# Sixty MLP units of a float32 decoder layer, from three matmuls per weight block to a two-matmul form with a PSUM bank of its own

## The chip, the core and the metric

The kernel runs on one core of a Trainium2 chip. The metric is the device time of one execution in microseconds (us): the median of several runs, beside runs of the kernel before. The engines are TensorE (PE in the profile, its weight loads PEld), VectorE (DVE), ScalarE (ACT) and SyncE (SP), which here issues the loads of weights. GpSimd does nothing.

## What is computed

One decoder layer on 256 tokens of width 2048, all in float32. The change lies in its last part, the MLP with a squared ReLU and a gated residual add:

```python
h2 = _modulate(_rms_norm(x, norm2_g[l]), shift2, scale2)
ff = jnp.square(jax.nn.relu(jnp.einsum("bsd,df->bsf", h2, w_ff1[l])))
x = x + gate2[:, None, :] * jnp.einsum("bsf,fd->bsd", ff, w_ff2[l])
return _rms_norm(x, final_g)
```

`w_ff1` is 2048 x 8192 and `w_ff2` 8192 x 2048.

## The kernel before

**Two halves of a float32.** TensorE is given float32 data rounded to its faster float32 form (`F32R`). To keep the precision, a number is held as a rounded part and the rest: ACT rounds (`w_round`, L178), DVE subtracts to get the rest (`w_rest`, L183). A product of weight and activation is then three products: rounded weight by rounded activation, rounded weight by the activation's rest, and the weight's rest by the rounded activation. The fourth is left out.

**Units.** A unit makes 128 output features for all 256 tokens. It has 16 blocks of 128 x 128 weights, one load of 1 MB, rounded and split in two halves of 128 x 1024 (`wh`, `wl`, four buffers each). There are two forms of it on TensorE:

- `gemm` (L196, matmuls at L204 to L206): three matmuls of 256 columns for each block, all added into one half of a PSUM bank (128 x 256 float32). 48 matmuls.
- `gemm_wide` (L221, matmuls at L229 to L232): one matmul of 512 columns takes the rounded weight to both halves of the activation at once, into both halves of a bank, and one of 256 columns adds the weight's rest to the first half. 32 matmuls. The result is the sum of the bank's halves. `join=True` adds them with an ACT copy (L236) and a DVE add (L237); with `join=False` the caller adds them to the residual with two DVE instructions.

**The MLP in four chunks.** Chunk c makes 16 tiles of `ff` (the first items, `ff1_unit`) and then adds what they give to the 16 tiles of the residual (`ff2_unit`). In the chunks c = 1, 2, 3 the first eight output tiles of the second product are not made in units but in summed steps (`sum_step`, matmuls at L1086 to L1088): a scheme that needs 7 products of blocks in place of 8, on sums of tokens (`token_sums`, L978 to L981) and sums of weights (`Item.sum`, L1010 to L1012). A step has 21 matmuls of 256 columns. There are 16 steps in a chunk; one stands behind each unit from f = 3 of the first items to f = 10 of the second product. The sums are held in PSUM for the whole chunk: 14 products, two to a bank, in the four banks of the pool `pa` and in three of the four banks of the pool `pg`. So while steps run, one bank is left for the units.

**The hand-written order.** In these chunks the function `mlp` (L1021) sets the order of all four engines; `pin` keeps it as the program order. `items` holds units and steps in the order of TensorE. While item i runs on TensorE, item i + 2 is rounded and split: `round` and `rest` of its first half, `round` and `rest` of its second half, and if the item behind it is a step, that step's sums of weights. Between these stand the three actions of the unit itself, `done[0]`, `done[1]` and `done[2]`. The rounding of a half waits until TensorE has used the buffer that it is written to: for a unit, those of the unit before (the first half when that is half done, the second half when it ends).

- A first item's actions are: ReLU out of PSUM into SBUF on ACT (L1137, `done[0]`, ahead of the second `round`), square and rounding on ACT (L1141, L1142, `done[1]`), the rest on DVE (L1146, `done[2]`, behind the second `rest`).
- A second item (f = 8, 9, 10) has one: its sum goes from PSUM into the residual (L1154, `done[2]`, behind the second `rest`).

The units f = 11 and up of the second product run outside `mlp`, in the common loop with a scheduler's order; f = 11 is a `gemm` too, f = 12 to 15 are wide or, at the very end, cut in pieces (`last_units`). `half_of` gives two neighbouring units the two halves of one bank (a bank each for f < 4 of the first items). Behind the third chunk DVE also joins the 14 sums (L1063, L1103, L1112) and squares are summed for the last norm (L157 to L161).

Of the kernel before, what the change touches and what calls it, by code (L numbers as in the profile page):

```python
# [10 lines left out]
F32 = mybir.dt.float32  # L11
# [55 lines left out]
def hybrid_layer(ctx: ExitStack, tc: tile.TileContext, x, xt, wada, w_p, w_r, w_f, vec, lruw, relb,  # L67
# [15 lines left out]
    def nm(s):  # L83
        cnt[0] += 1
        return f"{s}{cnt[0]}"
# [134 lines left out]

    def gemm_wide(parts, acts, join=True, out=None):  # L221

        ps = pg.tile([P, 2, T], F32, tag="pg", name=nm("pg"))
        n = len(acts)
        for k, hl in enumerate(acts):
            wh, wl = parts[k * P // WCH]
            w = slice(k * P % WCH, k * P % WCH + P)
            if k > 0:
                te.matmul(ps[:, 0], lhsT=wl[:, w], rhs=hl[:, 0], start=False, stop=False)  # L229
            te.matmul(ps, lhsT=wh[:, w], rhs=hl, start=k == 0, stop=k == n - 1)  # L230
            if k == 0:
                te.matmul(ps[:, 0], lhsT=wl[:, w], rhs=hl[:, 0], start=False, stop=False)  # L232
        if not join:
# [756 lines left out]
    class Item:  # L990
# [17 lines left out]
        def sum(self):  # L1008
            r = self.sums
            pin(ve.tensor_tensor(out=r[:, 4:6], in0=r[:, 1:3], in1=r[:, 0:1].broadcast_to((P, 2, T)), op=ALU.subtract))  # L1010
            pin(ve.tensor_tensor(out=r[:, 6], in0=r[:, 2], in1=r[:, 4], op=ALU.add))
            pin(ve.tensor_tensor(out=r[:, 7], in0=r[:, 6], in1=r[:, 3], op=ALU.subtract))  # L1012
# [8 lines left out]
    def mlp(items, ready, n):  # L1021
# [5 lines left out]
        for i, it in enumerate(items[:end]):  # L1027
# [4 lines left out]
            new.rest()  # L1032
            if not it.step and soon and soon.step:
                soon.sum()
            if not it.step:
                it.done[0](ps)
            new.round()
            if not it.step:
# [83 lines left out]

    hb = [None]

    def half_of(f, own=False):
        if own or f % 2 == 0:
            hb[0] = pg.tile([P, 2, T], F32, tag="pg", name=nm("pg"))
        return hb[0][:, f % 2]

    chunk = []  # L1130

    def first_item(c, f):
        t = {}

        def relu(ps):
            t[0] = tmp()
            pin(se.activation(t[0][:, 0], ps, AF.Relu))  # L1137

        def square(_):
            hl = ff[c, f] = pair(F32R)  # L1140
            pin(se.activation(t[0][:, 1], t[0][:, 0], AF.Square))  # L1141
            pin(se.activation(hl[:, 0], t[0][:, 1], AF.Copy))  # L1142
# [5 lines left out]
        def run(w):  # L1148
            return gemm(w, 0, [zn[k] for k in range(KT)], half_of(f, f < 4), pin)
        return Item(run, (relu, square, rest, [f // 2] if f % 2 else None), next_src())  # L1150

    def second_item(c, f):
        def out(ps):
            pin(ve.scalar_tensor_tensor(out=x1[f], in0=ps, scalar=mod[:, 5 * KT + f:5 * KT + f + 1], in1=x1[f],  # L1154
                                        op0=ALU.mult, op1=ALU.add))
            if c == 3:
                last_square(f)

        def run(w):
            return gemm(w, 0, [ff[c, j] for j in range(16)], half_of(f), pin)  # L1160
        return Item(run, (same, same, out, None), next_src())

# [115 lines left out]
    def ff2_unit(c, f):  # L1278
        def run(w):
# [5 lines left out]
            if c == 0:  # L1285
                flush(5 * KT + f + 1)
            acts = [ff[c, j] for j in range(16)]
            if c >= SUMMED_FROM and f < SUMMED * QUADS + 4:
                pss = [gemm(w, 0, acts, half_of(f))]
            else:  # L1290
                ps = gemm_wide(w, acts, join=False)
                pss = [ps[:, 0], ps[:, 1]]
            for ps in pss:
                ve.scalar_tensor_tensor(out=x1[f], in0=ps, scalar=mod[:, 5 * KT + f:5 * KT + f + 1], in1=x1[f],  # L1294
                                        op0=ALU.mult, op1=ALU.add)
# [179 lines left out]
```

## Time and profile before

| what | value |
|---|---|
| median of 3 runs | 1558.18 us (1557.3 to 1559.04) |
| the profiled execution: its time | 1556.84 us |
| the profiled execution: its span | 1555.0 us |
| granted TensorE clock | 0.999 |
| MLP chunks with steps, on TensorE | from 1008.75 us to the end |
| matmuls L204 (a third of all `gemm` matmuls) | x1838, of them x960 from 1008.5 us on |
| matmuls L230 (512 columns) | x1680, mean 394 ns from start to modelled end |

A row of the timeline gives the start, the duration, the engine, the line, the operation and its tiles, and in brackets how long the engine had been idle before it and what ended that. Matmuls overlap: the distance between the starts of two is what one costs, not its duration. The page's busy shares are means over stages with different limits; the argument below reads each stage by itself.

### The profile page before, as it was taken

The numbers are of one execution on the slowest core, as the hardware profiler recorded it, in microseconds if no ns is written. First come the engines' busy times: TensorE is split into PE (matmuls) and PEld (weight loads), VectorE is DVE, ScalarE is ACT, GpSimd is POOL, SyncE is SP. The second block draws the span as 40 slices with busy tenths as digits, with TensorE's granted clock in tenths as the row PEclk, the third lists the DMA queues.
The fourth block names the chain that finished last, engine by engine and source line by source line (L and its number), as shares of the span: only waits on it lengthen the run. The fifth ranks groups of instructions, "written<-read, shape, count | busy, mean of one in ns | idle before, by whom it ended". The sixth has DMA issues, their size and how long they took to land.

```text
span 1555.0 us, 28010 instructions
## 1 busy us (share of the span) xinstructions
PE 1536.9 (99%) x11225; PEld 1443.4 (93%) x11225; DVE 1314.1 (85%) x2059; ACT 928.0 (60%) x1517; POOL 0.2 (0%) x4
## 2 busy tenths in 40 slices
PE   8999999999999999999999999999999999999998
PEld 7999999999988888888889988899999999999997
DVE  5898988889899899999898877878876888778887
ACT  5753456657998664444466853356654666456655
POOL 0000000000000000000000000000000000000000
PEclk9999999999999999999999999999999999999999
DMA  9998976675777769988877667856664566546661
GB/s 374 365 379 309 367 279 242 210 257 176 260 255 248 249 220 343 353 298 313 334 269 261 231 243 259 323 190 195 191 225 163 177 202 197 212 142 198 203 208 64
DMA packets 108370, 388.09 MB, mean 250 GB/s; under 512 B 7920, under 2 KB 61520, under 8 KB 69584
## 3 DMA queue, kind: packets, MB, share of 16 engines
q1 hardware_dynamic: 103248, 381.51, 68.6%
q10 hardware_dynamic: 4992, 4.79, 1.0%
q8 instruction: 88, 1.44, 0.4%
q14 instruction: 42, 0.34, 0.1%
HBM read 384.13 MB, written 2.15 MB: 248 GB/s over the span
## 4 chain that ended last, share of the span: by engine, by line
PE 91%; ACT 3%; DVE 3%; DMA 2%; issue 1%; SPq 0%; DVEq 0%; ACTq 0%
PE pg L230 23%; PE pg L204 14%; PE pg L205 13%; PE pg L206 13%; PE pg L229 11%; DMA ra<-in_wada_dram 2%; ACT wh L178 1%; PE pa L1086 1%; PE pa L1088 1%; PE pa L1087 1%; DVE wl L183 1%; PE pg L1174 1%; PE pg L1173 1%; PE pg L1172 1%; PE pg L1087 1%
## 5 line engine op out<-in xcount | busy, mean ns | idle before, releaser
L183 DVE TENSOR_TENSOR wl<-rw,wh 128x1024 fp32r<-128x1024 f32 (+2 forms) x566 | 665.3, 1191 | 159.7 <-ACT wh L178 152.0
L178 ACT ACTIVATE wh<-rw 128x1024 fp32r<-128x1024 f32 (+2 forms) x566 | 574.3, 1030 | 368.0 <-PE pg L230 141.7
L230 PE MATMUL pg<-k,wh 128*128 128x512 f32 x1680 | 582.0, 394 | 0.6 <-DVE k L167 0.6
L204 PE MATMUL pg<-k,wh 128*128 128x256 f32 x1838 | 519.1, 283 | 3.5 <-DVE k L1154 3.5
L205 PE MATMUL pg<-k,wh 128*128 128x256 f32 x1838 | 515.4, 281 | 0.0
L206 PE MATMUL pg<-k,wl 128*128 128x256 f32 x1838 | 514.6, 280 | 0.0
L229 PE MATMUL pg<-k,wl 128*128 128x256 f32 x1575 | 441.6, 281 | 0.1
L230 PEld LDWEIGHTS pg<-k,wh 128*128 128x128 f32 x1680 | 309.0, 188 | 64.9 <-PE pg L230 0.9
L204 PEld LDWEIGHTS pg<-k,wh 128*128 128x128 f32 x1838 | 346.2, 188 | 9.9 <-issue 6.4
L206 PEld LDWEIGHTS pg<-k,wl 128*128 128x128 f32 x1838 | 346.1, 188 | 0.0
L205 PEld LDWEIGHTS pg<-k,wh 128*128 128x128 f32 x1838 | 345.8, 188 | 0.3
L229 PEld LDWEIGHTS pg<-k,wl 128*128 128x128 f32 x1575 | 296.2, 188 | 5.5 <-ACT k L166 1.0
L283 DVE CUSTOM_DVE_ANT_0 ra<-ra,scr,vc 128x2048 f32<-128x2048 f32 x96 | 225.2, 2346 | 6.7 <-DMA ra<-in_wada_dram 5.8
L1137 ACT ACTIVATE t<-pg 128x256 f32<-128x256 f32 x48 | 18.5, 385 | 91.2 <-PE pg L206 91.2
L236 ACT ACTIVATE t<-pg 128x256 f32<-128x256 f32 x79 | 29.0, 367 | 24.1 <-PE pg L230 24.1
L686 ACT ACTIVATE t<-t,as 128x128 f32<-128x128 f32 x64 | 28.4, 445 | 22.3 <-DVE as L683 22.3
L1172 PE MATMUL pg<-z,wh 128*128 128x258 f32 x144 | 40.8, 284 | 0.0
L1173 PE MATMUL pg<-z,wh 128*128 128x256 f32 x144 | 40.8, 284 | 0.0
L1174 PE MATMUL pg<-z,wl 128*128 128x258 f32 x144 | 40.7, 283 | 0.0
L237 DVE TENSOR_TENSOR t<-pg,t 128x256 f32<-128x256 f32 x79 | 33.0, 418 | 2.6 <-ACT t L236 2.6
L1294 DVE SCALAR_TENSOR_TENSOR k<-pg,mod,k 128x256 f32<-128x256 f32 x55 | 26.5, 482 | 10.0 <-PE pg L230 7.7
L1010 DVE TENSOR_TENSOR rw<-rw 128x512 f32<-128x512 f32 x48 | 32.9, 685 | 0.0
(241 smaller groups left out, 1641.7 us busy)
## 6 DMA issues: line engine op xcount, KB each, us to landing
rw<-in_w_f_dram SPq DMA_DIRECT2D x176, 1024.0 KB, 5.0
ra<-in_wada_dram SPq DMA_DIRECT2D x96, 1024.0 KB, 6.4
rw<-in_w_r_dram SPq DMA_DIRECT2D x30, 1024.0 KB, 5.1
rw<-in_w_p_dram SPq DMA_DIRECT2D x29, 960.0 KB, 6.7
rw<-in_w_f_dram SPq DMA_DIRECT2D x96, 256.0 KB, 3.2
bt<-ud ACTq DMA_DIRECT2D x8, 512.0 KB, 3.7
k<-in_w_p_dram SPq DMA_DIRECT2D x9, 256.0 KB, 10.8
lw<-in_lruw_dram SPq DMA_DIRECT2D x4, 512.0 KB, 5.8
```

The costliest lines, as they stand in the source:

```text
L178: pin(se.activation(wh[:, :c], raw[:, o:o + c], AF.Copy))
L183: pin(ve.tensor_tensor(out=wl[:, :c], in0=raw[:, o:o + c], in1=wh[:, :c].bitcast(F32), op=ALU.subtract))
L204: pin(te.matmul(ps, lhsT=wh[:, w], rhs=hl[:, 0], start=k == 0, stop=False))
L205: pin(te.matmul(ps, lhsT=wh[:, w], rhs=hl[:, 1], start=False, stop=False))
L206: pin(te.matmul(ps, lhsT=wl[:, w], rhs=hl[:, 0], start=False, stop=k == n - 1))
L229: te.matmul(ps[:, 0], lhsT=wl[:, w], rhs=hl[:, 0], start=False, stop=False)
L230: te.matmul(ps, lhsT=wh[:, w], rhs=hl, start=k == 0, stop=k == n - 1)
L237: ve.tensor_tensor(out=t, in0=ps[:, 0], in1=t, op=ALU.add)
L283: pin(ve.tensor_tensor_reduce(out=raw, in0=raw, in1=scr, scale=1.0, scalar=vc[:, V_BADA + c:V_BADA + c + 1], op0=ALU.mult, op1=ALU.add, ac ...
L1172: te.matmul(ps, lhsT=wh[:, e], rhs=z[k][:, 0:258], start=k == 0, stop=False)
L1173: te.matmul(ps[:, 0:256], lhsT=wh[:, e], rhs=z[k][:, 258:514], start=False, stop=False)
L1174: te.matmul(ps, lhsT=wl[:, e], rhs=z[k][:, 0:258], start=False, stop=k == KT - 1)
```

## The change

All units of the chunks 1 to 3 that used `gemm` now use `gemm_wide` with `join=False`: the 16 first items and f = 8 to 11 of the second product, 60 units in all. Each has a whole bank.

- A first item's `done[0]` is now the join: an ACT copy of the bank's second half to SBUF, then a DVE add of the first half. The ReLU moves to `done[1]`, from SBUF, with the square and the rounding behind it.
- A second item's evacuation is now `done[0]`, and is two DVE instructions in place of one.
- `Item.sum` is cut in two: the first instruction stays ahead of `done[0]`, the other two (`sum_more`) come behind it, both ahead of the second `rest`.
- `half_of` is gone.

```diff
-    def gemm_wide(parts, acts, join=True, out=None):
+    def gemm_wide(parts, acts, join=True, out=None, pin=same):
...
             if k > 0:
-                te.matmul(ps[:, 0], lhsT=wl[:, w], rhs=hl[:, 0], start=False, stop=False)
-            te.matmul(ps, lhsT=wh[:, w], rhs=hl, start=k == 0, stop=k == n - 1)
+                pin(te.matmul(ps[:, 0], lhsT=wl[:, w], rhs=hl[:, 0], start=False, stop=False))
+            pin(te.matmul(ps, lhsT=wh[:, w], rhs=hl, start=k == 0, stop=k == n - 1))
...
         def sum(self):
             r = self.sums
             pin(ve.tensor_tensor(out=r[:, 4:6], in0=r[:, 1:3], in1=r[:, 0:1].broadcast_to((P, 2, T)), op=ALU.subtract))
+
+        def sum_more(self):
+            r = self.sums
...
-            if not it.step and soon and soon.step:
+            ahead = not it.step and soon and soon.step
+            if ahead:
                 soon.sum()
             if not it.step:
                 it.done[0](ps)
+            if ahead:
+                soon.sum_more()
             new.round()
...
-        def relu(ps):
+        def joined(ps):
             t[0] = tmp()
-            pin(se.activation(t[0][:, 0], ps, AF.Relu))
+            pin(se.activation(t[0][:, 0], ps[:, 1], AF.Copy))
+            pin(ve.tensor_tensor(out=t[0][:, 0], in0=ps[:, 0], in1=t[0][:, 0], op=ALU.add))
 
         def square(_):
             hl = ff[c, f] = pair(F32R)
+            pin(se.activation(t[0][:, 0], t[0][:, 0], AF.Relu))
             pin(se.activation(t[0][:, 1], t[0][:, 0], AF.Square))
...
-            return gemm(w, 0, [zn[k] for k in range(KT)], half_of(f, f < 4), pin)
-        return Item(run, (relu, square, rest, [f // 2] if f % 2 else None), next_src())
+            return gemm_wide(w, [zn[k] for k in range(KT)], join=False, pin=pin)
+        return Item(run, (joined, square, rest, [f // 2] if f % 2 else None), next_src())
...
         def out(ps):
-            pin(ve.scalar_tensor_tensor(out=x1[f], in0=ps, scalar=mod[:, 5 * KT + f:5 * KT + f + 1], in1=x1[f],
-                                        op0=ALU.mult, op1=ALU.add))
+            for i in range(2):
+                pin(ve.scalar_tensor_tensor(out=x1[f], in0=ps[:, i], scalar=mod[:, 5 * KT + f:5 * KT + f + 1],
+                                            in1=x1[f], op0=ALU.mult, op1=ALU.add))
...
-            return gemm(w, 0, [ff[c, j] for j in range(16)], half_of(f), pin)
-        return Item(run, (same, same, out, None), next_src())
+            return gemm_wide(w, [ff[c, j] for j in range(16)], join=False, pin=pin)
+        return Item(run, (out, same, same, None), next_src())
...
-            if c >= SUMMED_FROM and f < SUMMED * QUADS + 4:
-                pss = [gemm(w, 0, acts, half_of(f))]
-            else:
-                ps = gemm_wide(w, acts, join=False)
-                pss = [ps[:, 0], ps[:, 1]]
-            for ps in pss:
+            ps = gemm_wide(w, [ff[c, j] for j in range(16)], join=False)
+            for i in range(2):
```

How the instructions stand in the queues, at three places. In these rows `rw` is a loaded weight tile (L183: the rest of a weight half; L1010 to L1015: sums of weights in place), `pg` and `pa` are PSUM banks, `t` and `k` SBUF tiles; the numbers tell one tile of a name from another.

The first place is VectorE in chunk 1, from the first half's rest of unit f = 15 (while f = 14 runs on TensorE) to the rest of `ff` for f = 14. Before:

```order
L183 TENSOR_TENSOR wl_12338<-rw_12145,wh_12336 128x1024
L1010 TENSOR_TENSOR rw_12176<-rw_12176 128x512
L1011 TENSOR_TENSOR rw_12176<-rw_12176 128x256
L1012 TENSOR_TENSOR rw_12176<-rw_12176 128x256
L183 TENSOR_TENSOR wl_12350<-rw_12145,wh_12345 128x1024
L1146 TENSOR_TENSOR k_12347<-t_12343,k_12347 128x256
```

And of the change:

```order
L183 TENSOR_TENSOR wl_12131<-rw_11967,wh_12129 128x1024
L1010 TENSOR_TENSOR rw_11998<-rw_11998 128x512
L1137 TENSOR_TENSOR t_12134<-pg_12096,t_12134 128x256
L1014 TENSOR_TENSOR rw_11998<-rw_11998 128x256
L1015 TENSOR_TENSOR rw_11998<-rw_11998 128x256
L183 TENSOR_TENSOR wl_12145<-rw_11967,wh_12139 128x1024
L1147 TENSOR_TENSOR k_12141<-t_12134,k_12141 128x256
```

The add of the join (L1137 of the change) is new in the queue. It stands behind the first of the three sums and ahead of the other two and of the second rest, and it needs ACT's copy, which needs the end of the unit.

The second place is VectorE in chunk 1 at the unit f = 8 of the second product, from the first half's rest of unit f = 9 on. Before:

```order
L183 TENSOR_TENSOR wl_12546<-rw_12353,wh_12544 128x1024
L1010 TENSOR_TENSOR rw_12384<-rw_12384 128x512
L1011 TENSOR_TENSOR rw_12384<-rw_12384 128x256
L1012 TENSOR_TENSOR rw_12384<-rw_12384 128x256
L183 TENSOR_TENSOR wl_12553<-rw_12353,wh_12551 128x1024
L1154 SCALAR_TENSOR_TENSOR k_8614<-pg_12495,mod,k_8614 128x256
```

And of the change:

```order
L183 TENSOR_TENSOR wl_12312<-rw_12148,wh_12310 128x1024
L1010 TENSOR_TENSOR rw_12179<-rw_12179 128x512
L1156 SCALAR_TENSOR_TENSOR k_8614<-pg_12277,mod,k_8614 128x256 x2
L1014 TENSOR_TENSOR rw_12179<-rw_12179 128x256
L1015 TENSOR_TENSOR rw_12179<-rw_12179 128x256
L183 TENSOR_TENSOR wl_12321<-rw_12148,wh_12319 128x1024
```

The evacuation, one instruction behind the second rest, has become two ahead of it, with two of the sums between them and that rest.

The third place is VectorE near the end, in chunk 3, from the first half's rest of unit f = 11 on (while f = 10 and the last step run on TensorE). `L1063`, in the change `L1069`, adds the chunk's sums from PSUM to those of the chunks before. Before:

```order
L183 TENSOR_TENSOR wl_16935<-rw_16758,wh_16933 128x1024
L1103 TENSOR_TENSOR scr<-scr 128x256 x3
L1063 TENSOR_TENSOR scr<-pa_15406,scr 128x512
L183 TENSOR_TENSOR wl_16939<-rw_16758,wh_16937 128x1024
L1154 SCALAR_TENSOR_TENSOR k_8719<-pg_16884,mod,k_8719 128x256
L1063 TENSOR_TENSOR k_12757<-pg_15407,k_12757 128x512
L161 TENSOR_TENSOR asq_16755<-asq_16755,t_16942 128x256
L1063 TENSOR_TENSOR k_12758<-pg_15408,k_12758 128x512
L1063 TENSOR_TENSOR k_12759<-pg_15409,k_12759 128x512
```

And of the change:

```order
L183 TENSOR_TENSOR wl_16120<-rw_15973,wh_16118 128x1024
L1069 TENSOR_TENSOR scr<-pa_14797,scr 128x512
L1156 SCALAR_TENSOR_TENSOR k_8719<-pg_16085,mod,k_8719 128x256
L1069 TENSOR_TENSOR scr<-pa_14798,scr 128x512
L1156 SCALAR_TENSOR_TENSOR k_8719<-pg_16085,mod,k_8719 128x256
L1069 TENSOR_TENSOR k_12495<-pg_14799,k_12495 128x512
L161 TENSOR_TENSOR asq_15964<-asq_15964,t_16124 128x256
L1069 TENSOR_TENSOR k_12496<-pg_14800,k_12496 128x512
L1069 TENSOR_TENSOR k_12497<-pg_14801,k_12497 128x512
L183 TENSOR_TENSOR wl_16130<-rw_15973,wh_16128 128x1024
```

Here the two evacuations of f = 10 have one of the sums' additions between them (it needs the last step's first three matmuls), and the second half's rest of f = 11, which stood ahead of the last three additions, stands behind them.

More of the change, by code (lines that the diff above doesn't have):

```diff
@@ L228, in gemm_wide @@
             if k > 0:
-                te.matmul(ps[:, 0], lhsT=wl[:, w], rhs=hl[:, 0], start=False, stop=False)
-            te.matmul(ps, lhsT=wh[:, w], rhs=hl, start=k == 0, stop=k == n - 1)
+                pin(te.matmul(ps[:, 0], lhsT=wl[:, w], rhs=hl[:, 0], start=False, stop=False))
+            pin(te.matmul(ps, lhsT=wh[:, w], rhs=hl, start=k == 0, stop=k == n - 1))
             if k == 0:
-                te.matmul(ps[:, 0], lhsT=wl[:, w], rhs=hl[:, 0], start=False, stop=False)
+                pin(te.matmul(ps[:, 0], lhsT=wl[:, w], rhs=hl[:, 0], start=False, stop=False))
         if not join:
@@ L1121, in last_square @@
         se.activation(x1[f], x1[f], AF.Copy, scale=vc[:, V_GF + f:V_GF + f + 1])
[L1123 to L1128, printed above, removed]
     chunk = []
@@ L1286, in run @@
                 flush(5 * KT + f + 1)
-            acts = [ff[c, j] for j in range(16)]
-            if c >= SUMMED_FROM and f < SUMMED * QUADS + 4:
-                pss = [gemm(w, 0, acts, half_of(f))]
-            else:
-                ps = gemm_wide(w, acts, join=False)
-                pss = [ps[:, 0], ps[:, 1]]
-            for ps in pss:
-                ve.scalar_tensor_tensor(out=x1[f], in0=ps, scalar=mod[:, 5 * KT + f:5 * KT + f + 1], in1=x1[f],
+            ps = gemm_wide(w, [ff[c, j] for j in range(16)], join=False)
+            for i in range(2):
+                ve.scalar_tensor_tensor(out=x1[f], in0=ps[:, i], scalar=mod[:, 5 * KT + f:5 * KT + f + 1], in1=x1[f],
                                         op0=ALU.mult, op1=ALU.add)
```

## Prediction

> **What bounds the kernel now.** The page comes first: the busy line, then the shares of the chain that ended last.
>
> ```profile
> PE 1536.9 (99%) x11225; PEld 1443.4 (93%) x11225; DVE 1314.1 (85%) x2059; ACT 928.0 (60%) x1517; POOL 0.2 (0%) x4
> ...
> PE 91%; ACT 3%; DVE 3%; DMA 2%; issue 1%; SPq 0%; DVEq 0%; ACTq 0%
> ```
>
> TensorE sets the end; only what shortens its own work or its waits can help. So I next asked the timeline for one unit of the old form, the step behind it, and the next unit:
>
> ```profile
> 1042.09 0.28 PE L204 MATMUL pg<-k,wh 128*128 128x256 f32 x1
> ...
> 1047.78 0.28 PE L1086 MATMUL pa<-wh,k 128*128 128x256 f32 x1
> ...
> 1050.25 0.28 PE L204 MATMUL pg<-k,wh 128*128 128x256 f32 x1
> ```
>
> The unit takes 1047.78 − 1042.09 = 5.69 us, its step 2.47 us, and nothing stands between them. A pair is 8.16 us. Units of the wide form run in the same trace behind the steps; the first matmul on the weight's rest (L232) starts once in each:
>
> ```profile
> 1169.36 0.28 PE L232 MATMUL pg<-k,wl 128*128 128x256 f32 x1
> ...
> 1174.93 0.28 PE L232 MATMUL pg<-k,wl 128*128 128x256 f32 x1
> ...
> 1341.46 0.28 PE L232 MATMUL pg<-k,wl 128*128 128x256 f32 x1
> ...
> 1347.08 0.28 PE L232 MATMUL pg<-k,wl 128*128 128x256 f32 x1
> ```
>
> 5.57 us in chunk 1, 5.62 us in chunk 2, for as many columns. Then the waits of TensorE from 1130 to 1350 us (two of the three chunk ends), and the place of the first:
>
> ```profile
> PE pg L204 <- DVE k L1154: 2.3, 6, 0.7
> ...
> 1137.47 0.29 PE L1086 MATMUL pa<-wh,k 128*128 128x256 f32 x1
> ...
> 1140.41 0.36 PE L204 MATMUL pg<-k,wh 128*128 128x256 f32 x1 [0.29 <-DVE k L1154]
> ...
> 1146.16 0.28 PE L1086 MATMUL pa<-wh,k 128*128 128x256 f32 x1
> ...
> 1137.55 1.06 ACT L178 ACTIVATE wh<-rw 128x1024 fp32r<-128x1024 f32 x1 [1.78 <-PE pg L205]
> ...
> 1138.64 1.23 DVE L183 TENSOR_TENSOR wl<-rw,wh 128x1024 fp32r<-128x1024 f32 x1
> ...
> 1139.79 0.48 DVE L1154 SCALAR_TENSOR_TENSOR k<-pg,mod,k 128x256 f32<-128x256 f32 x1
> ```
>
> At the second items TensorE does wait, for the unit before to leave the bank. The chain is plain: the unit ends at 1137.47, ACT rounds the second half until 1138.61, DVE makes its rest until 1139.87, then evacuates until 1140.27. That is 2.8 us behind the unit, and the step gives cover for 2.47. The step's slot grows to 2.94 us and the unit behind it from 5.69 to 5.75 us: 0.53 us where the view shows 0.29 us idle, so 0.24 us more than it shows. The two units lie in different halves of the bank, and still the second waits: here the bank is the unit of waiting.
>
> **Term 1, the wide form on TensorE.** Each unit goes from 5.69 to between 5.57 and 5.62 us: 0.07 to 0.12 us, I take 0.09 us. Sixty units change; the last three (f = 9 to 11 of chunk 3) belong to term 3. 57 x 0.09 = **5.1 us** (4.0 to 6.8).
>
> The Trainium skill, page "TensorE: Matmul & The Clock Gate", section "Back-to-back issue gap", gives the distance of isolated matmuls at full clock as their columns by 2.4 GHz plus some 2.5 ns. By that, an estimate, 16 matmuls fewer save 40 ns a unit, and the sum below would have 2.3 us in place of 5.1. The trace does not agree: it has 5.69 us for 48 matmuls of 256 columns, 119 ns each, where the page's formula gives 109.
>
> **Term 2, the waits at the ends of chunks 1 and 2.** The six idle stretches sum to 2.3 us, and each costs 0.24 us more than is shown: 2.3 + 6 x 0.24 = **3.7 us**, if the evacuation at `done[0]` comes in time. The next rows tell whether it does: load of two pairs of unit and step, DVE and ACT around a unit's end (1047.78), and durations of the new operations.
>
> ```profile
> 1042.09:1058.42 16.33, 16.33 (x141) 16.33 (x139) 14.01 (x22) 10.25 (x16) 0.00 (x0) 1.00 0.60 194
> ...
> 1047.24 0.69 DVE L1010 TENSOR_TENSOR rw<-rw 128x512 f32<-128x512 f32 x1
> 1047.96 0.43 DVE L1011 TENSOR_TENSOR rw<-rw 128x256 f32<-128x256 f32 x1
> 1048.42 0.43 DVE L1012 TENSOR_TENSOR rw<-rw 128x256 f32<-128x256 f32 x1
> 1049.34 1.22 DVE L183 TENSOR_TENSOR wl<-rw,wh 128x1024 fp32r<-128x1024 f32 x1 [0.49 <-ACT wh L178]
> 1050.48 0.42 DVE L1146 TENSOR_TENSOR k<-t,k 128x256 fp32r<-128x256 f32 x1
> 1050.82 0.28 DVE L978 SCALAR_TENSOR_TENSOR t<-t,t 128x128 f32<-128x128 f32 x1
> ...
> 1047.98 0.39 ACT L1137 ACTIVATE t<-pg 128x256 f32<-128x256 f32 x1 [1.91 <-PE pg L206]
> ...
> L236 ACT ACTIVATE t<-pg 128x256 f32<-128x256 f32 x79 | 29.0, 367 | 24.1 <-PE pg L230 24.1
> ...
> L237 DVE TENSOR_TENSOR t<-pg,t 128x256 f32<-128x256 f32 x79 | 33.0, 418 | 2.6 <-ACT t L236 2.6
> ...
> L1294 DVE SCALAR_TENSOR_TENSOR k<-pg,mod,k 128x256 f32<-128x256 f32 x55 | 26.5, 482 | 10.0 <-PE pg L230 7.7
> ```
>
> *The join of a first item.* ACT is idle when the unit ends (1.91 us in the row) and starts 0.20 us behind it; the copy takes 0.37, the add 0.42 us, so the bank is free 1.05 us behind the unit, with DVE through its first sum at 0.15 us. The step covers 2.47: a margin of 1.4 us. Where token sums (four instructions like L978, some 1.1 us of DVE) came before, DVE is up to 0.6 us later, and since it waited for ACT's copy anyway, the bank still comes at about 1.1. The first three units of a chunk have no step behind them, but the sums do not hold their banks yet, and four banks go round.
>
> *What is queued behind the add on DVE* is the other two sums, the second rest, and the steps' rests. The second rest ended at 1050.56, 2.8 us behind the unit; with the add to 1.05, the two sums in 0.9 and the rest in 1.22 us it ends at 3.2. The next unit needs it at its ninth block, 2.47 + 2.8 = 5.3 us behind. *On ACT* the ReLU is one instruction more (some 0.4 us, of 6.1 us free in two pairs), behind the round that others wait for.
>
> *The load of DVE.* Two pairs have 14.01 of 16.33 us; two adds make it 14.85, and TensorE's two pairs become 16.15. So TensorE stays the bound, and 1.3 us are left for the waits on ACT's copy, at most 0.5 us a pair where DVE is early, and none where it is late.
>
> *A second item.* Two instructions of 0.48 us from the end of the unit, or from the end of the first sum: the bank is free between 1.2 and 1.9 us behind. The cover is 2.47. Granted clock is 1.00 in the row, so nothing is to be had there.
>
> **Term 3, the last stretch.** Behind the first second item of chunk 3 DVE has much more to do (adding and joining the sums, squares):
>
> ```profile
> 1490.89 1.22 DVE L183 TENSOR_TENSOR wl<-rw,wh 128x1024 fp32r<-128x1024 f32 x1
> ...
> 1497.22 2.09 DVE L183 TENSOR_TENSOR wl<-rw,wh 128x1024 fp32r<-128x1024 f32 x2 [1.98 <-ACT wh L178]
> 1499.48 1.23 DVE L183 TENSOR_TENSOR wl<-rw,wh 128x1024 fp32r<-128x1024 f32 x1 [0.17 <-ACT wh L178]
> ...
> 1519.26 0.48 DVE L1294 SCALAR_TENSOR_TENSOR k<-pg,mod,k 128x256 f32<-128x256 f32 x1 [0.24 <-PE pg L206]
> ...
> 1533.93 0.43 DVE L161 TENSOR_TENSOR asq<-asq,t 128x256 f32<-128x256 f32 x1 [0.26 <-ACT t L160]
> 1534.27 1.22 DVE L183 TENSOR_TENSOR wl<-rw,wh 128x1024 fp32r<-128x1024 f32 x1
> ...
> 1492.45 0.28 PE L1086 MATMUL pa<-wh,k 128*128 128x256 f32 x1
> ...
> 1535.73 0.28 PE L1200 MATMUL pg<-k,wl 128*128 128x256 f32 x1
> 1537.63 0.40 PE L1208 MATMUL pg<-k,wh 128*128 128x256 f32 x2
> ```
>
> From 1490.89 to 1535.49 (44.6 us) DVE stands still for 1.98 + 0.17 + 0.24 + 0.26 = 2.65 us: 41.95 us of work, and its last piece, the rest of the last unit's second half, is wanted by L1200 from 1536.7 us on (halfway through 1.90 us). The change adds four evacuations of 0.48 us there and, by the order, leaves one sum of squares (0.4) for later: 43.5 us. It can reclaim part of the 1.98 us, since the evacuation no longer stands behind the round; about 1.1 us of waits remain. TensorE would be 2.2 us earlier: the three waits of this chunk end (as in chunk 1, 0.53 us or more each, 1.9 us) and 3 x 0.09. Counted from the unit's end at 1492.45, TensorE without waits comes to the second half of L1200 at 44.2 − 2.2 = 42.0 us; DVE, starting 0.3 us later, delivers at −1.56 + 0.3 + 43.5 + 1.1 = 43.3, plus 0.1 to be seen. So TensorE waits some 1.4 us there, and of 2.2 us **0.8 us** stay (0 to 2.2).
>
> **Sum.** 5.1 + 3.7 + 0.8 = 9.6 us. The profiled execution took 1556.84 us (span 1555.0); less 9.6 that is 1547.2. It stands 1.34 us under the median of 1558.18, so for the median I forecast 1558.18 − 9.6, **1548.5 us**. With the low ends (4.0, 2.5 where one wait in three stays, 0) it is 1551.7, with the high ones (6.8, 3.7, 2.2) 1545.5.
>
> **The rivals.**
>
> *The second items keep their wait.* The bank is free only when the second evacuation is through, and in chunks 2 and 3 additions of the sums (0.69 us each) stand between or ahead. If these come late, terms 2 and 3 fall to nothing and term 1 stays: 1553.1 us. Against it: 0.6 us of margin even at 1.9. Chance 0.08.
>
> *A new wait takes the place of none.* In before no first item waits, because its ReLU alone empties the bank, 0.6 us behind the unit. Now it takes two engines. If in every second pair, that with token sums, the add comes late enough to miss the step by as much as L1154 does today (0.47 us), then 20 x 0.47 = 9.4 us are given back: 1557.9 us, no change. Against it: 1.4 us of margin. Chance 0.11.
>
> *DVE becomes the bound of the pairs: slower.* Two pairs hold 14.85 us of DVE work, plus the waits for ACT's copy, which DVE pays in order. From 16.15 us on DVE sets the pace. If each add held DVE 1.0 us, the two pairs would take 14.85 + 2 x 1.0 = 16.85 us, 0.7 us more than TensorE's 16.15; 19.5 double pairs make 13.7 us: more than all the gain, 1558.18 − 9.6 + 13.7 = 1562.3 us. It needs each add to hold DVE for twice what the copy takes. Chance 0.07.
>
> That the evacuations are not ahead of the second rest can be left out: the order shows them there.
>
> **How the numbers follow.** Forecast 0.74, second items 0.08, no change 0.11, slower 0.07. The range takes in the forecast's own ends and the first rival, 1545.0 to 1554.0, and leaves out 0.18. Faster by over 0.2% (3.1 us, about what a measurement can tell from no change) are the forecast and the first rival: 0.82; within it 0.11; slower 0.07.
>
> **What would show it.** Right: wide units of 5.57 to 5.62 us from start to start in all three chunks; steps of 2.47 us behind f = 8 to 10 and no wait for the evacuation in chunks 1 and 2; DVE at about 14.85 us in two pairs of 16.15; a wait of TensorE for a weight's rest, or for the joined sums, of about 1.4 us behind 1500 us. Wrong: a TensorE wait for the add or the evacuation in steady pairs, ACT's copy held up behind a round, or wide units of 5.69 us.

## The result, and the profile after

The changed kernel took 1548.13 us (median of 4 runs, 1547.81 to 1550.78) beside 1558.26 us of the kernel before (4 runs, 1557.30 to 1559.04): a ratio of 0.9939, with a 95% interval of 0.9922 to 0.9956. That is 10.1 us less, where 9.6 were forecast. Run again on another occasion it had 1549.94 us (5 runs, 1547.91 to 1550.85) beside 1558.13, ratio 0.9945 (0.9932 to 0.9957), 8.2 us less. The profiled execution took 1547.82 us, span 1545.7, granted clock 0.999; by the spans it gained 9.3 us.

In the changed kernel some lines have other numbers: a step is now L1092 to L1094, the join L1136 (ACT) and L1137 (DVE), the evacuation of a second item L1156, that of the common loop L1291, and the matmuls of the last unit L1202 and L1210. The page of the changed kernel, busy line and shares of the chain that ended last:

```profile
PE 1530.2 (99%) x10265; PEld 1396.2 (90%) x10265; DVE 1330.8 (86%) x2119; ACT 944.8 (61%) x1565; POOL 0.2 (0%) x4
...
PE 94%; DVE 2%; ACT 2%; DMA 1%; issue 1%; SPq 0%; DVEq 0%; ACTq 0%
```

960 matmuls are gone, DVE has 17 us more, and the chain stands on TensorE for 94% of the span, not 91%. Next, the timeline of TensorE around the first second item of chunk 1: L1092 is the start of a step, L232 the second matmul of a unit.

```profile
1130.25 0.28 PE L232 MATMUL pg<-k,wl 128*128 128x256 f32 x1
1135.62 0.28 PE L1092 MATMUL pa<-wh,k 128*128 128x256 f32 x1
1138.34 0.28 PE L232 MATMUL pg<-k,wl 128*128 128x256 f32 x1
1143.71 0.28 PE L1092 MATMUL pa<-wh,k 128*128 128x256 f32 x1
1151.79 0.28 PE L1092 MATMUL pa<-wh,k 128*128 128x256 f32 x1
```

From step to step it is 8.09 and 8.08 us, that is 5.6 us for a wide unit behind its step of 2.48; in the kernel before it was 8.16 where nothing waited and 8.69 here. All waits of TensorE from 1000 us to the end (engine, tile and line, then what it waited for: us in total, times, longest):

```profile
PE pg L1202 <- DVE wl L183: 0.5, 2, 0.3
PE pg L1210 <- DVE k L1291: 0.3, 1, 0.3
```

No wait for the add or the evacuation is left in the three chunks; what is new stands in the last unit, and is on DVE. The distance between marks on TensorE gives the whole account. The marks are the starts of steps (behind f = 3, f = 8 and f = 10 of each chunk). The column "evacuation first" is the first experiment, below, and the last two columns are the last ones. The end of a span is known to 0.1 us, so the last row holds to about 0.05 us.

| stretch on TensorE, us | before | evacuation first | after | after, last four units in the old form | after, squares on GpSimd |
|---|---|---|---|---|---|
| chunk 1: step of f = 3 to step of f = 8 (13 units) | 106.01 | 106.01 | 105.00 | 105.00 | 105.00 |
| to the step of f = 10 (2 units) | 17.39 | 16.32 | 16.17 | 16.17 | 16.17 |
| to the first step of chunk 2 | 53.70 | 53.17 | 52.68 | 52.69 | 52.69 |
| chunk 2: the same three | 106.12 | 106.12 | 105.04 | 105.02 | 105.03 |
| | 17.85 | 16.34 | 16.13 | 16.14 | 16.13 |
| | 53.87 | 53.34 | 52.81 | 52.81 | 52.81 |
| chunk 3: the same, the last to the end of the span | 106.05 | 106.05 | 104.92 | 105.01 | 104.93 |
| | 17.81 | 16.31 | 16.16 | 16.31 | 16.15 |
| | 44.74 | 44.73 | 46.17 | 44.69 | 44.49 |

The first step of chunk 1 started at 1031.46 us before and at 1030.62 after; 0.39 us of this is the first four units of chunk 1 (22.71 and 22.32 us), and 0.45 us lies ahead of all changed code and is not counted for the change (in the kernels below with the same code up to there this step started anywhere from 1030.7 to 1031.8 us). The column of before with 1031.46 makes its span of 1555.0, that of after with 1030.62 its 1545.7.

The last row is the one that grew. TensorE at the end of the changed kernel (L1202 and L1210 are the two halves of the matmuls of the last unit in pieces; the distance between starts counts):

```profile
1520.70 1.11 PE L1202 MATMUL pg<-k,wl 128*128 128x256 f32 x8
1522.02 1.21 PE L1202 MATMUL pg<-k,wl 128*128 128x256 f32 x8 [0.21 <-DVE wl L183]
1523.07 2.06 PE L1210 MATMUL pg<-k,wh 128*128 128x256 f32 x16
1525.05 1.21 PE L1202 MATMUL pg<-k,wl 128*128 128x256 f32 x8
1526.53 1.22 PE L1202 MATMUL pg<-k,wl 128*128 128x256 f32 x8 [0.27 <-DVE wl L183]
1528.07 2.14 PE L1210 MATMUL pg<-k,wh 128*128 128x256 f32 x16 [0.32 <-DVE k L1291]
```

The first and the last of the same four pieces in the kernel before (L1200 and L1208 there):

```profile
1531.93 2.05 PE L1200 MATMUL pg<-k,wl 128*128 128x256 f32 x16
...
1537.63 3.24 PE L1208 MATMUL pg<-k,wh 128*128 128x256 f32 x26
```

From 1520.70 to 1528.07 it is 7.37 us, in the kernel before 5.70 us. TensorE gives back 1.67 us here, twice what the bracketed waits add up to.

### The profile page after: what moved, and what is told of

It reads as the page before. It is cut to its first block, busy times and chain, and to the rows that moved or that the text cites. A ratio compares the mean times of both kernels' runs of the same rounds, so it can differ in the third digit from the quotient of the medians.

```text
span 1545.7 us, 26101 instructions
## 1 busy us (share of the span) xinstructions
PE 1530.2 (99%) x10265; PEld 1396.2 (90%) x10265; DVE 1330.8 (86%) x2119; ACT 944.8 (61%) x1565; POOL 0.2 (0%) x4
## 3 DMA queue, kind: packets, MB, share of 16 engines
HBM read 384.13 MB, written 2.15 MB: 250 GB/s over the span
## 4 chain that ended last, share of the span: by engine, by line
PE 94%; DVE 2%; ACT 2%; DMA 1%; issue 1%; SPq 0%; DVEq 0%; ACTq 0%
PE pg L230 38%; PE pg L229 18%; PE pg L204 7%; PE pg L206 6%; PE pg L205 6%; PE pa L1094 1%; PE pa L1092 1%; PE pa L1093 1%; PE pg L232 1%; PE pg L1093 1%; PE pg L1092 1%; PE pg L1094 1%; PE pg L1176 1%; PE pg L1175 1%; PE pg L1174 1%; DMA ra<-in_wada_dram 1%
## 5 line engine op out<-in xcount | busy, mean ns | idle before, releaser
L230 PE MATMUL pg<-k,wh 128*128 128x512 f32 x2640 | 920.1, 394 | 0.6 <-DVE k L167 0.6
L178 ACT ACTIVATE wh<-rw 128x1024 fp32r<-128x1024 f32 (+2 forms) x566 | 573.9, 1030 | 345.8 <-PE pg L230 204.3
L183 DVE TENSOR_TENSOR wl<-rw,wh 128x1024 fp32r<-128x1024 f32 (+2 forms) x566 | 663.6, 1189 | 118.0 <-ACT wh L178 114.8
L229 PE MATMUL pg<-k,wl 128*128 128x256 f32 x2475 | 693.7, 280 | 0.0
L230 PEld LDWEIGHTS pg<-k,wh 128*128 128x128 f32 x2640 | 488.1, 188 | 101.3 <-PE pg L230 0.9
L229 PEld LDWEIGHTS pg<-k,wl 128*128 128x128 f32 x2475 | 465.6, 188 | 8.0 <-ACT k L166 0.7
L204 PE MATMUL pg<-k,wh 128*128 128x256 f32 x878 | 249.4, 284 | 0.0
L205 PE MATMUL pg<-k,wh 128*128 128x256 f32 x878 | 245.5, 280 | 0.0
L206 PE MATMUL pg<-k,wl 128*128 128x256 f32 x878 | 245.1, 280 | 0.0
L204 PEld LDWEIGHTS pg<-k,wh 128*128 128x128 f32 x878 | 165.0, 188 | 4.8 <-issue 4.7
L205 PEld LDWEIGHTS pg<-k,wh 128*128 128x128 f32 x878 | 165.0, 188 | 0.2
L206 PEld LDWEIGHTS pg<-k,wl 128*128 128x128 f32 x878 | 164.9, 188 | 0.0
L1136 ACT ACTIVATE t<-pg 128x256 f32<-128x256 f32 x48 | 18.4, 384 | 83.0 <-PE pg L230 83.0
L232 PE MATMUL pg<-k,wl 128*128 128x256 f32 x165 | 46.3, 280 | 0.0
L1291 DVE SCALAR_TENSOR_TENSOR k<-pg,mod,k 128x256 f32<-128x256 f32 x58 | 28.0, 482 | 9.5 <-PE pg L230 8.5
L232 PEld LDWEIGHTS pg<-k,wl 128*128 128x128 f32 x165 | 31.0, 188 | 4.9
```

Source lines behind the costliest of these rows:

```text
L178: pin(se.activation(wh[:, :c], raw[:, o:o + c], AF.Copy))
L183: pin(ve.tensor_tensor(out=wl[:, :c], in0=raw[:, o:o + c], in1=wh[:, :c].bitcast(F32), op=ALU.subtract))
L204: pin(te.matmul(ps, lhsT=wh[:, w], rhs=hl[:, 0], start=k == 0, stop=False))
L205: pin(te.matmul(ps, lhsT=wh[:, w], rhs=hl[:, 1], start=False, stop=False))
L206: pin(te.matmul(ps, lhsT=wl[:, w], rhs=hl[:, 0], start=False, stop=k == n - 1))
L229: pin(te.matmul(ps[:, 0], lhsT=wl[:, w], rhs=hl[:, 0], start=False, stop=False))
```

## The experiments

Nine runs followed, one of them the changed kernel again. Each was measured beside the kernel before on the same chip. Four were together (the kernel before: 1557.57 us, 15 runs, 1556.83 to 1560.62): the first three below and the one with the old form at the end. Four others were together too (1558.13, 9 runs). None leaves out work.

### Undo the wide form, keep the early evacuation

The kernel before, with one word moved: its second items are evacuated at `done[0]`, ahead of the second rest; units stay `gemm`, sums stay whole.

```diff
-        return Item(run, (same, same, out, None), next_src())
+        return Item(run, (out, same, same, None), next_src())
```

> The kernel before with one edit: the second items (f = 8 to 10) leave PSUM at done[0], ahead of the second rest, in one instruction; all units keep the form of three matmuls. Theory (the waits at the chunk ends come from the place of the evacuation alone): no wait of TensorE for the evacuation in any chunk, steps behind f = 8 to 10 of 2.47 us, units still 5.69 us; 3.7 us less in chunks 1 and 2 and 1.9 us less in chunk 3, where DVE has no work added: profiled execution 1551.2 us, median 1552.6 us, ratio to before 0.9964. Rival (TensorE waited for the rest of the weights, and the evacuation was only the last name in the queue): the slots stay at 2.94 us, time 1558 us, and the waits are put down to L183.

Measured: 1551.84 us (5 runs, 1551.50 to 1552.54), ratio 0.9958 (0.9946 to 0.9971), span 1549.7. TensorE has no wait from 1000 us to the end. The timeline of that kernel at the first second item of chunk 1, DVE and TensorE:

```profile
1137.32 0.29 PE L1086 MATMUL pa<-wh,k 128*128 128x256 f32 x1
...
1138.41 0.48 DVE L1154 SCALAR_TENSOR_TENSOR k<-pg,mod,k 128x256 f32<-128x256 f32 x1
1138.80 3.39 DVE L183 TENSOR_TENSOR wl<-rw,wh 128x1024 fp32r<-128x1024 f32 x3
...
1139.81 0.28 PE L204 MATMUL pg<-k,wh 128*128 128x256 f32 x1
```

The bank is free 1.57 us behind the unit in place of 2.8, with all three sums of weights still ahead, and the step takes 2.49 in place of 2.94. So it takes neither the wide form nor a bank for each unit to remove the waits at the chunk ends. The table's first two columns give what they were worth: 1.07 + 0.53 us in chunk 1, 1.51 + 0.53 in chunk 2, 1.50 in chunk 3. In chunk 3 the third wait is gone as well, but the last row stays (44.74 and 44.73): the 0.33 us that TensorE is earlier at the last unit are lost again there and behind it. The rest of the change's gain, the column "evacuation first" against the next, is the wide form.

### Keep the wide form, put the evacuation back

The changed kernel with that word moved back: wide units, two instructions of evacuation behind the second rest.

```diff
-        return Item(run, (out, same, same, None), next_src())
+        return Item(run, (same, same, out, None), next_src())
```

> The changed kernel with one edit: the second items' two evacuations stand at done[2], behind the second rest, as in the kernel before. Theory: the bank is free only 3.4 us behind the unit (second rest done at 2.4, two instructions of 0.48 us), so the slot of the step is 3.4 to 3.5 us in place of 2.47; six slots in chunks 1 and 2 cost 6 us, the three of chunk 3 some 1 to 3 us (part of that wait is there already, for DVE): 1555 to 1557 us, ratio to before 0.998 to 0.9995. Rival (the wide form alone made the gain, the place of the evacuation none): 1548 us.

Measured: 1559.78 us (11 runs, 1557.90 to 1562.40), ratio 1.0011 (1.0002 to 1.0020), span 1558.2. It is more than the theory had: the gain of 60 wide units, and a little more, is lost at eight places. The waits of TensorE from 1000 us on, then DVE behind the unit that ended at 1136.00:

```profile
PE pg L230 <- DVE k L1156: 5.7, 4, 1.9
PE pg L230 <- ACT wh L178: 1.9, 2, 1.0
PE pg L230 <- DVE k L1069: 1.5, 2, 1.0
```

```profile
1137.32 1.22 DVE L183 TENSOR_TENSOR wl<-rw,wh 128x1024 fp32r<-128x1024 f32 x1
1138.45 1.00 DVE L1156 SCALAR_TENSOR_TENSOR k<-pg,mod,k 128x256 f32<-128x256 f32 x2
```

The bank is free 3.45 us behind the unit; the step's slot is 3.60 us. (The row put down to the rounding L178 is of this kind too: that instruction ended at the same moment, but it rounds weights of a later step.) In chunks 2 and 3 an addition of the sums (L1069, 0.68 us) comes between, and the wait behind f = 9 is 1.92 and 1.86 us. There is a second price: the unit behind each of these two took 7.23 and 7.22 us, not 5.59. The first matmul behind the wait of 1.92 us, and then two stretches of TensorE from there on (columns: length, busy time and matmuls, granted clock, DMA share, GB/s):

```profile
1326.03 0.70 PE L230 MATMUL pg<-k,wh 128*128 128x512 f32 x1 [1.92 <-DVE k L1156]
```

```profile
1326.03:1329.50 3.47, 3.47 (x11) 0.51 0.92 314
1329.50:1333.00 3.50, 3.50 (x22) 1.00 0.64 267
```

The granted clock was 0.51 for 3.5 us, and 1.00 again behind that. That is 1.6 us on top of the wait, twice. The same units in the stretch to the step of f = 10 took 18.48, 21.06 and 21.01 us in the three chunks, where the changed kernel has 16.17, 16.13 and 16.16: 12.1 us, nearly all of the 12.5 us between the two spans.

### Put the add of the first items late

The changed kernel with the DVE add of the join at `done[2]`, behind the second rest, where the evacuation was; ReLU, square, rounding, `ff`'s rest and the token sums follow, one item later.

```diff
...
+            if behind:
+                behind.pop().done[4](None)
...
+        def square(ps):
+            hl = ff[c, f] = pair(F32R)
             pin(ve.tensor_tensor(out=t[0][:, 0], in0=ps[:, 0], in1=t[0][:, 0], op=ALU.add))
-
-        def square(_):
-            hl = ff[c, f] = pair(F32R)
...
-        return Item(run, (joined, square, rest, [f // 2] if f % 2 else None), next_src())
+        return Item(run, (joined, same, square, [f // 2] if f % 2 else None, rest), next_src())
```

> The changed kernel with the join's DVE add behind the second rest (ACT's copy stays where it is), and the rest of ff and the token sums one item later so that they hold nothing up. Theory (the bank must be empty within the step's 2.47 us): the second rest ends 2.8 us behind the unit, the add at 3.2, so each slot behind f = 4 to 15 takes 3.3 us in place of 2.47, and the unit behind it 0.06 more: 36 x 0.9 = 32 us, profiled execution about 1580 us, with TensorE waits named by the add. Rival (where the add stands does not matter to TensorE, because the bank is not what it waits for): 1548 us.

Measured, in a single run: 1626.48 us, span 1624.7, where about 1580 were expected. TensorE's waits in it (the add is L1144 here), and the end of an add behind the unit that ended at 1104.13:

```profile
PE pg L230 <- DVE t L1144: 44.5, 36, 1.6
PE pa L1096 <- ACT ts L986: 16.0, 3, 5.4
```

```profile
1106.60 1.22 DVE L183 TENSOR_TENSOR wl<-rw,wh 128x1024 fp32r<-128x1024 f32 x1
1107.73 0.42 DVE L1144 TENSOR_TENSOR t<-pg,t 128x256 f32<-128x256 f32 x1
```

36 of the 39 steps behind first items now wait for the bank. It is free 4.02 us behind the unit, and the step's slot is 4.16; in every second unit 3.59 and 3.73. Over 2.48 us each, the 36 slots sum to 50 us, of 79 us between the spans. Some 22 of the others were no part of the question: three first steps wait 5.3 us for token sums that the edit made an item later, and then run at a lower granted clock (9.85 us in the first). The 50 us are the price of a bank that comes free late behind every first item; the second rival of the prediction had it late by less, and in every second pair.

### Sums first

The changed kernel with `soon.sum_more()` moved ahead of `done[0]`: all three sums ahead of join and evacuation, the second rest still behind.

```diff
             if ahead:
                 soon.sum()
+                soon.sum_more()
             if not it.step:
                 it.done[0](ps)
-            if ahead:
-                soon.sum_more()
```

> The changed kernel, with all three sums of weights ahead of the join or evacuation, as in the kernel before; the second rest still behind. The bank comes free some 0.75 us later: 1.8 us behind a first item's unit in place of 1.03, 2.0 to 2.3 behind a second item's. Theory (the step's 2.47 us cover all that comes sooner): no wait and no change, 1548 us, ratio to the changed kernel 1.000. Rival (a wait starts earlier than the step's end, or VectorE's place matters otherwise): some 0.3 us for each of 48 units, 1560 us.

Measured: 1550.06 us (4 runs, 1549.83 to 1550.23), ratio 0.9948 (0.9934 to 0.9961); the changed kernel beside it 0.9945 (0.9932 to 0.9957). The times do not tell the two apart. The profile shows where this half of the change's order matters. At the first items the add ends 1.59 us behind the unit, and the three stretches of 13 units have 105.00, 105.03 and 104.93 us: not a wait among them. At the second items there are two waits, in chunks 2 and 3, where none was expected:

```profile
PE pg L230 <- DVE k L1155: 1.8, 1, 1.8
PE pg L230 <- ACT wh L178: 0.2, 1, 0.2
```

The long one is the first rival's mechanism. These are DVE's rows behind the unit that ended at 1493.13 (L1068 adds the sums, L1155 evacuates):

```profile
1488.94 4.37 DVE L183 TENSOR_TENSOR wl<-rw,wh 128x1024 fp32r<-128x1024 f32 x4 [1.98 <-ACT wh L178]
1493.22 0.69 DVE L1010 TENSOR_TENSOR rw<-rw 128x512 f32<-128x512 f32 x1
1494.04 0.69 DVE L1068 TENSOR_TENSOR scr<-pa,scr 128x512 f32<-128x512 f32 x1
...
1494.98 0.69 DVE L1068 TENSOR_TENSOR scr<-pa,scr 128x512 f32<-128x512 f32 x1
...
1495.91 0.48 DVE L1155 SCALAR_TENSOR_TENSOR k<-pg,mod,k 128x256 f32<-128x256 f32 x1
1496.30 0.68 DVE L1068 TENSOR_TENSOR scr<-pa,scr 128x512 f32<-128x512 f32 x1
1496.90 0.48 DVE L1155 SCALAR_TENSOR_TENSOR k<-pg,mod,k 128x256 f32<-128x256 f32 x1
```

DVE was late at the start already (1.98 us for the rounding: on ACT the square of f = 8 stands ahead of that and waits for the evacuation). Then three additions of the sums slip in, and the bank is free 4.25 us behind the unit. Part of it comes back, because TensorE waits for DVE in the last stretch anyway: the two units take 19.1 us in place of 16.2, and what follows 44.4 in place of 46.2. With 0.15 and 0.6 us at the second items of chunks 1 and 2 this order is some 2 us slower by the marks, less than the timed runs can tell here.

### VectorE's load: one more, three more

The changed kernel, with the rest of each first item in the chunks 1 to 3 computed four times (twice in the second kernel) into the same place.

```diff
-            pin(ve.tensor_tensor(out=ff[c, f][:, 1], in0=sq[f], in1=ff[c, f][:, 0].bitcast(F32), op=ALU.subtract))
+            for _ in range(4):
+                pin(ve.tensor_tensor(out=ff[c, f][:, 1], in0=sq[f], in1=ff[c, f][:, 0].bitcast(F32), op=ALU.subtract))
```

> The changed kernel, with the rest of each first item of chunks 1 to 3 computed four times in place of once: three more instructions of 0.34 us on VectorE for each unit, behind the second rest. VectorE's work in two pairs of unit and step goes from 14.50 to 16.54 us, and with its waits for the copy (0.28 us each) to between 16.5 and 17.1, where TensorE needs 16.15. Theory (VectorE sets the pace from 16.15 us on): 19.5 double pairs by 0.4 to 0.95 us make 8 to 18 us, 1556 to 1566 us, and the wait appears at a rounded rest (L183) or at the join. Rival (VectorE has more slack than the busy share shows): no change, 1548.

> The changed kernel, with the rest of each first item of chunks 1 to 3 computed twice: one more instruction of 0.34 us on VectorE for each unit, where three more made 18 waits of TensorE for the join of 0.43 to 0.60 us. VectorE's work in two pairs goes from 14.50 to 15.18 us, under TensorE's 16.15. Theory (the work of the pair decides, from 16.15 us on): no wait at the join, the stretch from the first step of a chunk to the step behind f = 15 stays at 96.9 us, and 1548 us. Rival (VectorE's slack is used up already, so that every instruction counts): a third of the cost of three, 4.8 us from the 4.8 us a chunk that those cost, 1553 us.

Measured, a single run each: 1568.53 us with three more, 1548.26 us with one more (the kernel before beside it 1560.06). First two pairs of unit and step of the changed kernel, then of the one with one more, then two pairs of the one with three more (columns: length, then busy time and instructions of PE, PEld, DVE, ACT and POOL, granted clock, DMA share, GB/s):

```profile
1041.17:1057.38 16.21, 16.21 (x109) 14.79 (x108) 14.50 (x24) 11.00 (x18) 0.00 (x0) 1.00 0.61 195
```

```profile
1041.17:1057.38 16.21, 16.21 (x109) 14.79 (x108) 15.19 (x27) 11.10 (x18) 0.00 (x0) 1.00 0.61 195
```

```profile
1043.31:1060.28 16.97, 16.44 (x106) 14.84 (x106) 16.66 (x30) 11.19 (x18) 0.00 (x0) 1.00 0.56 185
```

With 15.19 us of DVE in 16.21 nothing waits: 105.00, 105.03 and 104.93 us for the three stretches of 13 units (in chunk 3 one second item's unit took 5.93 us in place of 5.59, with no wait that the view names). With 16.66 us the two pairs take 16.97 us, and TensorE waits 18 times for the add of the join, 0.43 to 0.60 us, in every second pair, that behind the token sums. So the work of the pair decides, as the third rival had it, and from about the length of TensorE's own two pairs on: between 15.19 and 16.66 us. The price came out a little above the 8 to 18 us that were expected, since second items (three waits, 3.7 us in all) were hit as well.

### The last stretch, seen from both sides

The forecast had TensorE wait for DVE at the end. Two kernels test whether DVE's load there is the cause. In the first the last four units with a changed form (f = 8 to 11 of chunk 3) go back to `gemm`, in half of a bank of their own, with one evacuation instead of two; the rest of the change stays.

```diff
-            for i in range(2):
+            for i in range(1 if c == 3 else 2):
...
+            if c == 3:
+                ps = pg.tile([P, 2, T], F32, tag="pg", name=nm("pg"))
+                gemm(w, 0, [ff[c, j] for j in range(16)], ps[:, 0], pin)
+                return ps
             return gemm_wide(w, [ff[c, j] for j in range(16)], join=False, pin=pin)
...
```

(The lines left out do the same for f = 11 in the common loop.)

> The changed kernel, but in chunk 3 the units f = 8 to 11 have the old form of three matmuls (in the first half of a bank of their own) and one evacuation, at done[0]. Theory (the last stretch is bound by DVE's work): 4 evacuations of 0.4 us less on DVE, 4 x 0.09 us more on TensorE; the 1.8 us that TensorE loses to waits between the two last rest parts (L1202) and behind them shrink to 0.2 to 0.5 us: 1.0 to 1.3 us less than the changed kernel, 1546.9 us. Rival (these waits come from the order of the queues or from ACT, not from DVE's load): 0.4 us more, 1548.5 us.

In the second, DVE's adds of squares (L161) in chunk 3 go to GpSimd, which had nothing to do.

```diff
...
-            ve.tensor_tensor(out=asq, in0=asq, in1=q, op=ALU.add)
+            (eng or ve).tensor_tensor(out=asq, in0=asq, in1=q, op=ALU.add)
...
-        sumsq(stat[3], x1[f], first)
+        sumsq(stat[3], x1[f], first, nc.gpsimd)
```

> The changed kernel, with the adds of squares (L161) of chunk 3 on GpSimd in place of VectorE. Theory (VectorE's work is what TensorE waits for behind 1520 us: 0.21 + 0.27 us shown, 1.76 us by the distance from 1520.70 to 1531.24 against 8.78 in the kernel before): some twelve adds of 0.34 us leave VectorE, the wait goes, 1546.5 us, that is 1.5 us less than the changed kernel beside it. Rival (the wait has another cause, as the rounding on ScalarE): no change, 1548. A second way to lose it: the adds are so slow on GpSimd that the last of them ends behind TensorE, then 1548 or more, with the last norm waiting for GpSimd.

> The changed kernel again, as the base for the runs beside it. All theories: 1547 to 1549 us.

Measured: 1547.24 us with the old form at the end (5 runs, 1546.67 to 1547.66; ratio 0.9927, 0.9915 to 0.9940), 1546.32 us with the squares on GpSimd (5 runs, 1545.94 to 1547.68; ratio 0.9925, 0.9912 to 0.9939), 1549.94 us for the changed kernel beside the latter. In both traces TensorE has no wait behind 1000 us. Its four pieces at the end, with the old form and then with the squares on GpSimd (there L1206 and L1214 are what is L1202 and L1210 elsewhere):

```profile
1522.19 2.06 PE L1206 MATMUL pg<-k,wl 128*128 128x256 f32 x16
...
1528.09 3.31 PE L1214 MATMUL pg<-k,wh 128*128 128x256 f32 x26
```

```profile
1521.17 2.06 PE L1202 MATMUL pg<-k,wl 128*128 128x256 f32 x16
...
1526.85 3.24 PE L1210 MATMUL pg<-k,wh 128*128 128x256 f32 x26
```

5.90 and 5.68 us, against 7.37 in the changed kernel and 5.70 before. Four evacuations less (4 x 0.48 us) take away most of the loss and a dozen adds less all of it, with TensorE's and ACT's work as it was in the second kernel. So DVE's load there was the cause. In the table's last row the old form saves about 1.5 us, but it pays 0.09 + 0.15 us in the rows above for three of its four longer units; the squares on GpSimd save about 1.65 us and pay nothing on TensorE. No run of these two kernels is as long as the shortest of the changed kernel's nine (1547.81 us), though the intervals of the ratios overlap; which of the two is faster the times do not tell.

## Why the prediction was right

- **What bounds it.** TensorE without waits in the steady pairs, as the prediction had it: one more instruction on DVE in each pair cost nothing.
- **Term 1, 57 wide units, 5.1 us forecast.** From the column "evacuation first" to the next, with the first four units of chunk 1: 0.39 + 1.01 + 0.15 + 0.49 + 1.08 + 0.21 + 0.53 + 1.13 = 4.99 us, that is 0.088 us a unit where 0.09 was taken. The estimate from the Trainium skill ("TensorE: Matmul & The Clock Gate", "Back-to-back issue gap"), 0.04 us a unit, is ruled out by this.
- **Term 2, the waits at the ends of chunks 1 and 2, 3.7 us.** The first experiment alone has 1.07 + 0.53 + 1.51 + 0.53 = 3.64 us. The six stretches of idle time showed 2.3 us; the other 0.24 us for each, read at the first wait, came out right for the six together.
- **Term 3, 0.8 us kept of 2.2.** The mechanism was right, DVE's load with four more evacuations, as both experiments on the last stretch show; a size was off. Counted from the step of f = 8, TensorE came to the last unit 2.15 us earlier (39.48 to 37.33), where 2.2 were forecast. DVE delivered the last rest 43.10 us behind that mark, where 43.3 were forecast, and TensorE was held 1.1 us by it, where 1.4 were forecast. What the forecast left out stands behind that rest: the last piece waited for an evacuation too (L1291, 0.32 us in brackets, 0.6 by the distance), and the matmuls behind it took 0.3 us longer. So about 2 us were lost in place of 1.4, and of the two rows of chunk 3 from the step of f = 8 on 62.55 − 62.33 = 0.2 us stayed.
- **The sum.** 4.99 + 3.64 + 0.22 = 8.9 us by the marks, 9.6 forecast; the spans differ by 9.3 because 0.45 us lay ahead of the changed code. The two timed comparisons, 10.1 and 8.2 us, stand on both sides. That the spans came within 0.3 us of the forecast is partly luck: the 0.6 us missing in term 3 and the 0.45 us ahead of the changed code nearly cancel.
- **The join.** Forecast 1.05 us behind the unit, second rest done at 3.2. The rows of the changed kernel behind the unit that ended at 1046.78:

```profile
1046.98 0.38 ACT L1136 ACTIVATE t<-pg 128x256 f32<-128x256 f32 x1 [1.73 <-PE pg L230]
1047.39 0.42 DVE L1137 TENSOR_TENSOR t<-pg,t 128x256 f32<-128x256 f32 x1 [0.29 <-ACT t L1136]
1048.53 1.22 DVE L183 TENSOR_TENSOR wl<-rw,wh 128x1024 fp32r<-128x1024 f32 x1
```

  1.03 and 2.97 us. DVE did wait for the copy, 0.29 us here, and it cost nothing. Its work in two pairs was 14.50 us, not 14.85.
- **The rivals.** The margin that spoke against the second one, 1.4 us, is real, and the runs give it a scale. The bank came free 1.03 us behind a first item's unit in the changed kernel, 1.59 with the sums first, both without a wait. It came 2.42 us behind f = 8 of chunk 3 with the sums first (slot 2.57), 2.80 in the kernel before (2.94), 3.13 with three more on DVE (3.18), 3.59 and 4.02 with the late add (3.73 and 4.16). So the unit behind starts 0.05 to 0.15 us after the bank is free, or when the step's 2.48 us are over, whichever is later. The first rival's mechanism, additions of the sums in front of the evacuation, appeared with the sums first, and an addition between the two evacuations made the wait longer in the kernel with the late evacuation. The third needs more than one further instruction on DVE in each pair.

## What to carry to other kernels

Where a bank is handed from unit to unit, measure two numbers: how far behind a unit's end the bank is free, and what TensorE has to do in between. Moving the evacuation ahead of one long vector instruction was worth about as much here as removing 16 of 48 matmuls from each of 60 units, and without it the second would have gained nothing. At the end of a kernel ask which engine is the last to finish: in this kernel instructions that are free in the steady state were paid there in full, and an idle engine could take others off the busy one.

## What the runs showed that was not expected

- **Behind waits of just under 2 us the clock was lower.** Behind TensorE's wait of 1.92 us the granted clock was 0.51 over 3.5 us, as shown above; behind that of 1.86 us it was 0.64 and then 0.87 over 3.5 us each, which is together about the same loss, 1.7 us (second and third row here). Behind the wait of 1.76 us in the kernel with sums first it stayed at 1.00 (first row). In the kernel with the late add it was 1.00 over 3.5 us behind a wait of 1.51 us, and the units behind its 33 waits of 1.06 to 1.56 us took no more than some 5.7 us; behind the first of its three waits of over 5 us it was 0.50 (1038.30 to 1041.80 us).

```profile
1497.50:1500.90 3.40, 3.38 (x19) 1.00 0.05 19
```

```profile
1506.00:1509.50 3.50, 3.48 (x14) 0.64 0.64 262
1509.50:1513.00 3.50, 3.50 (x19) 0.87 0.61 183
```

  The Trainium skill ("TensorE: Matmul & The Clock Gate", "Part 1: The HAM clock gate") gives an idle window of about 3.4 us as the condition; here a little more than half of that sufficed. The halving itself agrees with the page (0.51 and 0.50). Whether a length between 1.76 and 1.86 us is a limit, or the place of the wait decides, stays open: only three waits lie near it.
- **GpSimd's adds and VectorE's subtractions held each other up.** In the kernel with the squares on GpSimd, four rests L183 took 4.63 us where GpSimd stood still, and two took 3.36 us beside its adds, 1.7 in place of 1.2 us each:

```profile
1503.90 4.63 DVE L183 TENSOR_TENSOR wl<-rw,wh 128x1024 fp32r<-128x1024 f32 x4 [0.18 <-ACT wh L178]
...
1517.24 3.36 DVE L183 TENSOR_TENSOR wl<-rw,wh 128x1024 fp32r<-128x1024 f32 x2
```

```profile
1502.52 0.74 POOL L161 TENSOR_TENSOR asq<-asq,t 128x256 f32<-128x256 f32 x1 [8.07 <-ACT t L160]
1510.25 4.82 POOL L161 TENSOR_TENSOR asq<-asq,t 128x256 f32<-128x256 f32 x1 [6.99 <-ACT t L160]
1516.29 11.75 POOL L161 TENSOR_TENSOR asq<-asq,t 128x256 f32<-128x256 f32 x10 [1.22 <-ACT t L160]
```

  An add took 0.74 us beside VectorE's additions out of PSUM (first row), but one took 4.82 us while VectorE ran its additions from SBUF to SBUF (L1109), eleven of which kept their 0.42 to 0.43 us, and the ten in a row took 11.75 us. Spans on GpSimd are rough, and the runs do not show what the two engines share.
  The move still paid: 12 adds of 0.42 us left DVE behind 1500 us, and though DVE then waited 1.26 us for the last of them, TensorE did not.
- **Time lost ahead is not always lost.** With the sums first TensorE lost 2.9 us at the second items of chunk 3 and had 1.7 of them back at the end, where it would have waited for DVE.
